# Round 1's first head: both weight groups in turn, seven products each

## The chip, the core and the metric

The kernel runs on one core of a Trainium2 chip. TensorE multiplies matrices into PSUM banks; VectorE (DVE in the profile), ScalarE (ACT) and GpSimd (POOL) work elementwise; SyncE (SP) issues the transfers between memory and the core. Each engine takes its instructions in the order in which the program lists them for it, and waits on semaphores for the others. The metric is the device time of one execution in microseconds, the median of several runs.

## The reference

A decoder layer on 2048 positions (and 16 learned meta tokens ahead of them) of width 1024. In all matters here:

```python
hn = rms_norm(h, norm_g)
proj = hn @ w_in                        # 1024 -> 8 x 512: cx, cb, cc, cg, q, k, v, rg
conv_out = short_conv_branch(cx, cb, cc, conv_w) * silu(cg)
ret = head_group_norm(retention_chunkwise(rotary(q) * d**-0.5, rotary(k), v), ret_norm_g)
mixed = concat([conv_out, ret * silu(rg)])
h = rms_norm(h + mixed @ w_out, final_g)
```

The retention has four heads of 128 and works in chunks of 128 positions; the convolution branch is worked in four groups of 128 channels.

## The kernel before

**Rounds and units.** The positions are worked in two rounds of 1024 (`r` = 0, 1). A round goes through eight units (`UNITS`): four heads (`head`) and four convolution groups (`conv_group`; the first of round 0 is `group_plain`). Each unit has two weight groups of four 128x512 blocks. For a head these are keys and values, then queries and the output gate. Round 0 ends with the convolution group 7, round 1 starts with head 0.

**Three matmuls for one.** All operands are fp32 and are split into a rounded high part and a remainder. `split` does it: ScalarE casts the high part (`wh` for a weight, `mh` for an activation), VectorE subtracts it from the source (`wl`, `ml`). Each 128x128 by 128x512 product then takes three matmuls, low by high, high by low, high by high.

**Seven products for eight.** `quad` multiplies a 2x2 block of weights by a 2x2 block of activations with seven block products instead of eight. A product is four steps along the depth of three matmuls each, 12 matmuls. It needs four activation blocks (`m[0]` to `m[6]`, one slot for each; some are inputs x, others sums T of x blocks which were worked out and stored during round 0 and are loaded again) and one weight block. Weight splits go through a ring of three buffers (`RING`), so a weight can be split only when the product three before it is done. `take` adds up the results in two PSUM banks. In round 1 the weight sums of most groups are loaded from `sums_a`, where round 0 stored them: seven blocks for a group and not four. `quad_plain` is the direct form with eight products, 96 matmuls, from four weight blocks that have a slot of their own.

**Head 0 of round 1.** The loop at the end (`else` branch, L1139 on) loads and scales all sixteen x blocks (`moving`), splits four plain weight blocks, and loads the sums of two slots. `head` works keys and values with `quad_plain`, as `first` holds something there; it then loads the sums of the other slots (`rest_of_sums`), stores the last convolution group's result (`kept`), and works queries and gate with `quad`. After a result of keys or queries is in (`take`), `rotary` turns it on VectorE in four steps, two of them on half of the partitions. Values and keys are split into 16-bit planes on ScalarE, transposed by a transfer, and joined again (`part`, `join`, `join_keys`).

**The order.** The code names the work; a scheduler places it on each engine by readiness and by the order of the code, and `tc.issue_after` keeps a piece behind a named instruction. In the texts below, K0 to K6 and Q0 to Q6 are the seven products of the key-value and the query group of this head in their new form, and L0 to L6 the products of the last weight group of round 0.

Of the kernel before, what the change touches and what calls it, by code (L numbers as in the profile page):

```python
# [8 lines left out]
F32 = mybir.dt.float32  # L9
# [6 lines left out]
P = 128  # L16
# [6 lines left out]
HB = 512  # L23
# [3 lines left out]
KH = KT // 2  # L27
# [51 lines left out]
def hybrid_trunk(ctx: ExitStack, tc: tile.TileContext, t, out: bass.AP, chunk_decay):  # L79
# [47 lines left out]
    def add(eng, out, a, b):  # L127
        eng.tensor_tensor(out=out, in0=a, in1=b, op=ALU.add)  # L128
# [53 lines left out]
    def moving(load, scale=None, after={}, behind={}):  # L182
# [11 lines left out]
                    after.get((j, k), lambda: None)()  # L194
        return m, blocks

    def block_sums(b11, b12, b22, b21, t1, t3, f, g):
# [14 lines left out]
        sub(nc.vector, t3, b22, b11)  # L212
# [10 lines left out]

    loaded = [None]

    def prepared(m, src, ns, held={}):

        for n in ns:
            for kt in range(KH):
                a = held.get((n, kt))  # L230
                if a is None:
                    a = gen("t")[:, :HB]
                    loaded[0] = nc.sync.dma_start(a, src[n, kt])
                parts(m, SUMS[n], kt, a)

    def idle():
# [4 lines left out]
    def quad(w, m, take, steps=()):  # L241


        steps = iter(steps)

        def product(i, bank, first):
            (wh, wl) = w[i]
            for kt in range(KH):
                ks = slice(kt * P, (kt + 1) * P)
                mh, ml = m[i][kt]  # L250
                for n, (a, b) in enumerate(((wl, mh), (wh, ml), (wh, mh))):
                    nc.tensor.matmul(  # L252
                        bank, a[:, ks], b, start=first and kt == 0 and n == 0, stop=kt == KH - 1 and n == 2,
                        skip_group_check=not first,
                    )
# [29 lines left out]
        take(1, 0, xb, None)  # L285

    def plain_part(n, load, slot):
        a = sb.tile([P, HB], F32, name="ra", tag="ra", bufs=RAW)
# [175 lines left out]
    def load_x(r):  # L464
        def load(k, j):
            a = gen("x")[:, :HB]
            if r == 0:
                in_line(a, t["xT"][r, j, k])
            else:
                nc.sync.dma_start(a, t["xT"][r, j, k])  # L470
            return a

        return load
# [76 lines left out]
    def w_loads(n, r=0):  # L550
# [4 lines left out]
        return [lambda a, b=b: nc.sync.dma_start(a, b) for b in blocks]  # L555

    def kept_sums(n, r):
        return sums_a[n] if r == 0 and n in KEPT else None

    mixed = [  # L560
        dram.tile([2, 2, 2, P, KH, P], F32, name=f"mixed{b}", tag=f"mixed{b}") for b in range(SEQ // HB)
# [87 lines left out]
    def conv_group(g, r, m, f, blocks, ahead, steps=(), last=False):  # L649
# [34 lines left out]
        cs = [taps(u[j], g) for j in range(2)]  # L684
        gates = []

        def gated():
            j, c = gates.pop()
            nc.scalar.activation(c, c, AF.Silu)  # L689
            mul(nc.gpsimd, cs[j], cs[j], rr[j])  # L690
            mul(nc.gpsimd, cs[j], cs[j], c)

        def take(i, j, pp, c):
            if i == 0:
                add(nc.vector, c, pp, c)
# [8 lines left out]
            taken[0] = nc.vector.tensor_tensor(out=cs[j], in0=pp, in1=cs[j], op=ALU.mult)  # L704
# [4 lines left out]
        def store():  # L709
            for j in range(2):  # L710
                store_mixed(r, j, g, cs[j])

        if last:
            kept.append(store)
        else:
            store()
        return blocks
# [23 lines left out]
    def part(a, to_cross=None):  # L741

        apart, across = gen("pl")[:, :HB], gen("tr")[:, :HB]
        nc.scalar.copy(out=planes(apart), in_=halves(a))
        if to_cross is None:
            cross(across, apart)
        else:
            to_cross.append((across, apart))
        return across

    waiting = [[], []]

    def catch_up(stage):

# [10 lines left out]
    def head(h, r, m, rot_t, f, turning, blocks, ahead, sums, first=(), between=((), idle, idle, idle)):  # L765
# [1 line left out]

        to_cross, queried = [], []  # L770
# [5 lines left out]
        def take(i, j, pp, c):  # L776
            if i == 1 and c is None:
                v[j] = part(pp, to_cross if len(first) else None)
                return
            d = gen("kv")[:, :HB]  # L780
            if c is None:
                nc.scalar.copy(out=d, in_=pp)
            else:
                add(nc.vector, d, pp, c)
            if i == 0:
                rotary(d, tables[j])
                k[j] = d
            else:
                v[j] = d
                late.append(j)  # L790

        if len(first) > 0:
            quad_plain(first[0], m, take)
        else:
            with tc.issue_after(spreading[0].ins) if r + h == 0 else nullcontext():
                w = stationary(blocks[0], nc.vector if r + h == 0 else nc.gpsimd, kept_sums(2 * h, r))
            quad(w, m, take, between[0] or (finish_late,))
            catch_up(0)
        between[1]()
        if to_cross:  # L800
            with tc.issue_after(loaded[0].ins):
                for pair in to_cross:
                    cross(*pair)
        q, sg = [None, None], [None, None]

        def take(i, j, pp, c):
            d = gen("qg")[:, :HB]
            if i == 0:
                if c is None:
                    nc.scalar.copy(out=d, in_=pp)  # L810
                else:
                    add(nc.vector, d, pp, c)
                rotary(d, tables[j])
# [11 lines left out]
        def split_keys(j):  # L825
            across_k[j] = part(k[j])
# [5 lines left out]
        def split_late():  # L832
            for j in late:
                v[j] = part(v[j])
            split_keys(0)

        def join(j):
# [15 lines left out]
            join_keys(0)  # L853
            between[3]()

        quad(stationary(load_raw(w_loads(2 * h + 1, r)), keep=kept_sums(2 * h + 1, r)), m, take, (split_late, middle, late_middle))
        with tc.issue_after(copied[0].ins):
            join(1)
            weigh(1)
            join_keys(1)  # L860
        between[2]()
        with tc.issue_after(queried[0].ins):
            next(sums, None)
# [191 lines left out]
    for r in range(NR):  # L1055
# [7 lines left out]
        if r == 0:  # L1063
# [70 lines left out]
                            parts(m, i, kt, held[kt])  # L1134

            between = (), idle, idle, idle
            later = prepare(load_x(1), sums_x, gain_of)
        else:
            m, b = moving(load_x(r), gain_of)  # L1139
            first = [plain_parts(w_loads(0))]  # L1140
            load_tables()
            prepared(m, sums_x, (1, 3))

            def rest_of_sums():
                prepared(m, sums_x, (0, 2))
                with tc.issue_after(loaded[0].ins):
                    kept.pop()()

            between = (), rest_of_sums, idle, idle
# [74 lines left out]
```

## Time and profile before

| | |
|---|---|
| median of 3 runs | 867.62 us (867.51 to 868.01) |
| profiled execution | 867.66 us, of which the span is 865.9 |
| weight loads (PEld) | 705.7 us busy |
| VectorE | 683.0 us busy |
| ScalarE | 499.0 us busy |
| GpSimd | 288.7 us busy |
| DMA | 154.43 MB, mean 178 GB/s |

The span is the time from the first to the last instruction of the profiled execution. A busy time is a sum over an engine's instructions, which overlap with those of other engines. The page also cuts the span into 40 slices of 21.6 us; the digits are tenths of a slice:

```profile
PE   8999999999999999999999999999999999999996
DVE  6798989889897977979677787976655699767663
ACT  7875648474855654948374757544433565555553
DMA  8736357566777744966365657547344584455441
```

The change touches the seventeenth to nineteenth slice, from about 345 to 410 us.

### The profile page before, as it was taken

The numbers are of one execution on the slowest core, as the hardware profiler recorded it, in microseconds if no ns is written. First come the engines' busy times: TensorE is split into PE (matmuls) and PEld (weight loads), VectorE is DVE, ScalarE is ACT, GpSimd is POOL, SyncE is SP. The second block draws the span as 40 slices with busy tenths as digits, with TensorE's granted clock in tenths as the row PEclk, the third lists the DMA queues.
The fourth block names the chain that finished last, engine by engine and source line by source line (L and its number), as shares of the span: only waits on it lengthen the run. The fifth ranks groups of instructions, "written<-read, shape, count | busy, mean of one in ns | idle before, by whom it ended". The sixth has DMA issues, their size and how long they took to land.

```text
span 865.9 us, 12846 instructions
## 1 busy us (share of the span) xinstructions
PE 854.1 (99%) x4216; PEld 705.7 (82%) x4216; DVE 683.0 (79%) x1204; ACT 499.0 (58%) x901; POOL 288.7 (33%) x226
## 2 busy tenths in 40 slices
PE   8999999999999999999999999999999999999996
PEld 6778888878887778788888888888888888888885
DVE  6798989889897977979677787976655699767663
ACT  7875648474855654948374757544433565555553
POOL 0022232422255554320000002341312154777773
PEclk9999999999999999999999999999999999999999
DMA  8736357566777744966365657547344584455441
GB/s 294 252 142 159 96 145 210 149 185 193 183 233 242 243 147 158 338 197 163 81 171 178 162 194 167 186 135 256 97 122 122 205 318 146 162 181 169 146 139 68
DMA packets 141187, 154.43 MB, mean 178 GB/s; under 512 B 59904, under 2 KB 77632, under 8 KB 141120
## 3 DMA queue, kind: packets, MB, share of 16 engines
q1 hardware_dynamic: 140544, 153.21, 57.8%
q8 instruction: 33, 0.54, 0.3%
q10 hardware_dynamic: 576, 0.40, 0.1%
q14 instruction: 34, 0.28, 0.1%
HBM read 101.14 MB, written 39.85 MB: 163 GB/s over the span
## 4 chain that ended last, share of the span: by engine, by line
PE 93%; DVE 3%; issue 1%; DMA 1%; POOL 0%; ACT 0%; POOLq 0%; SPq 0%; DVEq 0%
PE pj L252 75%; PE pj L309 5%; PE pj L333 5%; PE ms L902 2%; PE ms L891 2%; PE ms L901 2%; PE ms L878 2%; PE ms L506 1%; DVE wl L120 1%; DMA ra<-in_w_in 1%; DVE ml L123 0%; DMA gain<-in_norm_g 0%; DVE qg L931 0%; DVE x L205 0%; DVE c L581 0%
## 5 line engine op out<-in xcount | busy, mean ns | idle before, releaser
L252 PE MATMUL pj<-mh,wl 128*128 128x512 f32 x1008 | 395.7, 393 | 0.5 <-DVE wl L120 0.5
L252 PE MATMUL pj<-mh,wh 128*128 128x512 f32 x1008 | 393.2, 390 | 0.0
L252 PE MATMUL pj<-ml,wh 128*128 128x512 f32 x1008 | 392.7, 390 | 0.0
L119 ACT CAST wh<-ra 128x512 fp32r<-128x512 f32 x229 | 142.3, 621 | 250.3 <-PE pj L252 210.6
L120 DVE TENSOR_TENSOR wl<-ra,wh 128x512 fp32r<-128x512 f32 x229 | 188.3, 824 | 59.4 <-ACT wh L119 58.2
L252 PEld LDWEIGHTS pj<-mh,wl 128*128 128x128 f32 x1008 | 189.3, 188 | 41.1 <-issue 1.1
L252 PEld LDWEIGHTS pj<-mh,wh 128*128 128x128 f32 x1008 | 189.3, 188 | 39.4
L252 PEld LDWEIGHTS pj<-ml,wh 128*128 128x128 f32 x1008 | 189.4, 188 | 38.1
L131 POOL TENSOR_TENSOR ra<-ra 128x512 f32<-128x512 f32 x44 | 69.0, 1567 | 78.7 <-PE ms L506 38.3
L914 POOL TENSOR_TENSOR rp<-rs,neg_half 128x4 f32<-128x4 f32 x16 | 18.8, 1173 | 151.5 <-DVE rs L128 151.4
L259 ACT COPY tc<-pj 128x512 f32<-128x512 f32 x108 | 62.6, 580 | 0.2
L128 POOL TENSOR_TENSOR sa<-ra 128x512 f32<-128x512 f32 x22 | 33.2, 1508 | 59.2 <-DMA ra<-in_w_in 38.2
L663 POOL TENSOR_TENSOR c<-c,tc 128x512 f32<-128x512 f32 x14 | 26.1, 1862 | 47.7 <-ACT tc L689 47.7
L131 POOL TENSOR_TENSOR ra<-sa,ra 128x512 f32<-128x512 f32 x22 | 31.7, 1440 | 30.5 <-DVE wl L120 20.6
L977 DVE TENSOR_TENSOR yo<-pj,yo 128x512 f32<-128x512 f32 (+1 forms) x33 | 21.9, 671 | 17.5 <-PE pj L252 8.8
L663 POOL TENSOR_TENSOR c<-c,rr 128x512 f32<-128x512 f32 x14 | 22.3, 1592 | 36.9 <-DVE c L704 25.0
L988 POOL TENSOR_TENSOR z<-yo,final_g 128x512 f32<-128x512 f32 x16 | 27.1, 1692 | 19.4 <-DVE yo L977 19.4
L128 DVE TENSOR_TENSOR tc<-pj,tc 128x512 f32<-128x512 f32 x28 | 19.2, 684 | 14.6 <-PE pj L252 14.6
L918 DVE TENSOR_SCALAR pm<-ms,mv,rp 128x128 f32<-128x128 f32 x64 | 21.8, 404 | 10.2 <-POOL rp L914 10.2
L123 DVE SCALAR_TENSOR_TENSOR ml<-x,gain,mh 128x512 fp32r<-128x512 f32 x32 | 24.7, 809 | 5.6 <-ACT mh L122 5.4
L128 POOL TENSOR_TENSOR yo<-yo,tc 128x512 f32<-128x512 f32 x18 | 26.0, 1454 | 3.4 <-ACT tc L259 3.2
L581 DVE SCALAR_TENSOR_TENSOR c<-u,conv_w,c 128x512 f32<-128x512 f32 x32 | 25.2, 830 | 2.3 <-POOL u L572 1.2
(161 smaller groups left out, 1214.0 us busy)
## 6 DMA issues: line engine op xcount, KB each, us to landing
ra<-in_w_in SPq DMA_DIRECT2D x111, 256.0 KB, 2.9
ra<-sums_a SPq DMA_DIRECT2D x52, 256.0 KB, 2.9
x<-in_xT SPq DMA_DIRECT2D x48, 256.0 KB, 5.0
sums_a<-ra SPq DMA_DIRECT2D x42, 256.0 KB, 2.1
w<-in_w_out SPq DMA_DIRECT2D x32, 256.0 KB, 5.0
ra<-mixed SPq DMA_DIRECT2D x32, 256.0 KB, 2.8
yo<-in_x SPq DMA_DIRECT2D x32, 256.0 KB, 4.4
ra<-in_x SPq DMA_DIRECT2D x16, 256.0 KB, 3.5
```

Source lines behind the costliest of these rows:

```text
L119: nc.scalar.copy(out=hi, in_=src)
L120: lowered[0] = eng.tensor_tensor(out=lo, in0=src, in1=hi.bitcast(F32), op=ALU.subtract)
L123: nc.vector.scalar_tensor_tensor(out=lo, in0=src, scalar=scale, in1=hi.bitcast(F32), op0=ALU.mult, op1=ALU.subtract)
L128: eng.tensor_tensor(out=out, in0=a, in1=b, op=ALU.add)
L131: eng.tensor_tensor(out=out, in0=a, in1=b, op=ALU.subtract)
L252: nc.tensor.matmul(bank, a[:, ks], b, start=first and kt == 0 and n == 0, stop=kt == KH - 1 and n == 2, skip_group_check=not first,)
L259: copied[0] = nc.scalar.copy(out=c, in_=bank)
L309: nc.tensor.matmul(banks[i], a[:, ks], b, start=half + kt + n == 0, stop=half == 1 and kt == KH - 1 and n == 2,)
L333: nc.tensor.matmul(banks[n][i], a[:, ks], b, start=half + kt + s == 0, stop=half == 1 and kt == KH - 1 and s == 2,)
L581: nc.vector.scalar_tensor_tensor(out=c, in0=u[:, tap : tap + HB], scalar=conv_w[:, g, tap : tap + 1], in1=c, op0=ALU.mult, op1=ALU.add)
L663: eng.tensor_tensor(out=out, in0=a, in1=b, op=ALU.mult)
L988: nc.gpsimd.tensor_tensor(out=ys[i][j], in0=y, in1=final_g[:, j * HB : (j + 1) * HB], op=ALU.mult)
```

## The change

Keys and values of round 1's first head are worked in seven products like all the others, and in turn with the queries: K0, Q0, K1, Q1 and so on, two banks for each of the two groups. The new function `quads` does it; `weights_in_turn` loads each weight block just ahead of its split, and `moving_in_turn` loads only the twelve x blocks that seven products need. All these loads stand in one line (`in_line`), in the order of their use. The steps between the pairs of products prepare the blocks of later ones.

```diff
+    def moving_in_turn(load, scale, sums):
...
+        blocks(0, 0)
+        with tc.issue_after(copied[0].ins):
+            blocks(1, 0)
+        steps = [
+            lambda: sums(m, 1), lambda: sums(m, 0), lambda: sums(m, 2), lambda: blocks(1, 1), lambda: sums(m, 3),
+        ]
+        return m, steps
...
+    def quads(ws, m, takes, between=()):
...
+        for i in range(7):
+            for n, take in enumerate(takes):
+                if i < 2:
+                    banks[n][i] = ps_proj()
+                bank = banks[n][1 if i in (1, 3, 5) else 0]
+                product(n, i, bank, i in (0, 1, 3))
+                if i == 0:
+                    copies[n] = copy(bank)
+                elif i == 1:
+                    take(0, 0, bank, copies[n])
...
+            next(between, idle)()
...
+    def weights_in_turn(n, r):
+        for load in w_loads(n, r, in_line):
+            a = raw()
+            load(a)
+            yield weight_parts(a)
```

In `conv_group` the last group of round 0 no longer gates its result at once. `gate_late` does it, and it is called after the blocks of T2 are split, with two GpSimd products where there were four:

```diff
+        def gate_late():
+            for j, gate in enumerate(ungated):
+                mul(nc.vector, gate, gate, rr[j])
+                nc.scalar.activation(gate, gate, AF.Silu)
+                mul(nc.vector, cs[j], cs[j], rr[j])
+                mul(nc.gpsimd, cs[j], cs[j], gate)
+            return store
...
-            m, b = moving(load_x(r), gain_of)
-            first = [plain_parts(w_loads(0))]
+            m, first = moving_in_turn(load_x(r), gain_of, lambda m, n: prepared(m, sums_x, (n,), in_turn=True))
             load_tables()
-            prepared(m, sums_x, (1, 3))
-
-            def rest_of_sums():
-                prepared(m, sums_x, (0, 2))
+
+            def open_sums(t2=first[0], t1=first[1]):
+                t2()
+                with tc.issue_after(lowered[0].ins):
+                    store_kept = kept.pop()()
+                t1()
+                early.append(lowered[0])
+                return store_kept
```

`early` keeps the first rotary of keys and of queries behind the T1 blocks (`m[3]`). In `head`, the transposes of values and keys and the joins move with it, to behind the products:

```diff
+        if len(first) > 0:
+            steps = first[:3] + [lambda: (first[3](), split_keys(0)), idle, split_values, lambda: split_keys(1)]
+            quads([weights_in_turn(2 * h + n, r) for n in range(2)], m, (take_keys, take_queries), steps)
+            join_keys(0)
+            join(1)
+            weigh(1)
+            join(0)
+            weigh(0)
+            join_keys(1)
```

Where the instructions stand shows at two places. On TensorE at the seam of the rounds, where `pj_3735` is a bank of the last group and `pj_4040` one of the plain keys, the order before was:

```order
L252 MATMUL pj_3735<-ml43_747,wh_3719 128x512
L252 MATMUL pj_3735<-mh43_746,wh_3719 128x512
L309 MATMUL pj_4040<-mh00_3871,mh30_3967 128x512
L309 MATMUL pj_4040<-mh00_3871,ml30_3968 128x512
L309 MATMUL pj_4040<-ml00_3872,mh30_3967 128x512
```

The first 24 matmuls of the plain keys stood between L4 and L5. Now:

```order
L272 MATMUL pj_3735<-ml43_747,wh_3719 128x512
L272 MATMUL pj_3735<-mh43_746,wh_3719 128x512
L272 MATMUL pj_3806<-mh50_275,wl_3728 128x512
L272 MATMUL pj_3806<-ml50_276,wh_3727 128x512
L272 MATMUL pj_3806<-mh50_275,wh_3727 128x512
```

L5 follows L4 directly, and K0 comes after L6. The second place is VectorE between Q1 and K2, where `qg_4057` is the addition that reads the bank of Q1, `kv_4031` are the keys, `ml4` are blocks for K4 and Q4, and `wl_4091` is the weight of K2. The rows now:

```order
L128 TENSOR_TENSOR qg_4057<-pj_4038,tc_3954 128x512
L816 TENSOR_TENSOR kv_4031<-kv_4031,rot_4033 128x512
L813 TENSOR_TENSOR rot_4059<-qg_4057,rot_t_3862 64x512
L814 TENSOR_TENSOR rot_4059<-qg_4057,rot_t_3862 64x512
L120 TENSOR_TENSOR ml40_4067<-t_4064,mh40_4066 128x512
L815 TENSOR_TENSOR qg_4057<-qg_4057,rot_t_3862 128x512
L120 TENSOR_TENSOR ml41_4073<-t_4070,mh41_4072 128x512
L120 TENSOR_TENSOR ml42_4079<-t_4076,mh42_4078 128x512
L816 TENSOR_TENSOR qg_4057<-qg_4057,rot_4059 128x512
L120 TENSOR_TENSOR ml43_4085<-t_4082,mh43_4084 128x512
L120 TENSOR_TENSOR wl_4091<-ra_4088,wh_4090 128x512
```

Before, at the addition of the query group's product 1 (`qg_4286`), the weights of the products 2, 3 and 4 (the last is `wl_4243`) stood ahead of it:

```order
L120 TENSOR_TENSOR wl_4239<-ra_4218,wh_4238 128x512
L120 TENSOR_TENSOR ml32_4175<-t_4172,mh32_4174 128x512
L120 TENSOR_TENSOR ml33_4181<-t_4178,mh33_4180 128x512
L120 TENSOR_TENSOR ml40_4187<-t_4184,mh40_4186 128x512
L120 TENSOR_TENSOR wl_4243<-ra_4220,wh_4242 128x512
L120 TENSOR_TENSOR ml41_4193<-t_4190,mh41_4192 128x512
L128 TENSOR_TENSOR qg_4286<-pj_4273,tc_4267 128x512
```

So the weight of the next product has moved from ahead of that addition to ten rows behind it.

More of the change, by code (lines that the diff above doesn't have):

```diff
@@ L195, in moving, with blocks @@
         return m, blocks
+    def moving_in_turn(load, scale, sums):
+        m = [[] for _ in range(8)]
+        def blocks(half, j):
+            for kt in range(KH):
+                k = half * KH + kt
+                parts(m, BLOCK[half][j], kt, load(k, j), scale(k) if scale else None)
+        blocks(0, 0)
[5 more added lines that the diff above has]
+        return m, steps
     def block_sums(b11, b12, b22, b21, t1, t3, f, g):
@@ L224, in hybrid_trunk, with prepared @@
     loaded = [None]
-    def prepared(m, src, ns, held={}):
+    def prepared(m, src, ns, held={}, in_turn=False):
         for n in ns:
@@ L232, in prepared @@
                     a = gen("t")[:, :HB]
-                    loaded[0] = nc.sync.dma_start(a, src[n, kt])
+                    if in_turn:
+                        in_line(a, src[n, kt])
+                    loaded[0] = line[0] if in_turn else nc.sync.dma_start(a, src[n, kt])
                 parts(m, SUMS[n], kt, a)
@@ L285, in quad, with product, copy @@
         take(1, 0, xb, None)
+    def quads(ws, m, takes, between=()):
+        between = iter(between)
+        banks = [[None, None] for _ in ws]
+        copies = [None for _ in ws]
+        def product(n, i, bank, first):
+            wh, wl = next(ws[n])
+            for kt in range(KH):
+                ks = slice(kt * P, (kt + 1) * P)
+                mh, ml = m[i][kt]
+                for s, (a, b) in enumerate(((wl, mh), (wh, ml), (wh, mh))):
+                    nc.tensor.matmul(
+                        bank, a[:, ks], b, start=first and kt == 0 and s == 0, stop=kt == KH - 1 and s == 2,
+                        skip_group_check=not first,
+                    )
+        def copy(bank):
+            c = sb.tile([P, HB], F32, name="tc", tag="tc", bufs=COPIES)
+            copied[0] = nc.scalar.copy(out=c, in_=bank)
+            return c
+        for i in range(7):
[8 more added lines that the diff above has]
+                    take(0, 0, bank, copies[n])
+                elif i == 2:
+                    copies[n] = [copy(bank)]
+                elif i == 3:
+                    copies[n].append(copy(bank))
+                elif i == 4:
+                    take(1, 1, bank, copies[n][1])
+                elif i == 5:
+                    take(0, 1, bank, copies[n][0])
+                else:
+                    take(1, 0, bank, None)
+            next(between, idle)()
     def plain_part(n, load, slot):
@@ L462, in in_line, with load_x @@
             line[0] = nc.sync.dma_start(out, src)
-    def load_x(r):
+    def load_x(r, first=True):
         def load(k, j):
             a = gen("x")[:, :HB]
-            if r == 0:
+            if first:
                 in_line(a, t["xT"][r, j, k])
@@ L548, in hybrid_trunk, with w_loads @@
     KEPT = [n for n in range(4 * NG) if n // 2 != NG]
-    def w_loads(n, r=0):
+    def w_loads(n, r=0, load=nc.sync.dma_start):
         if r and n in KEPT:
@@ L554, in w_loads @@
             blocks = [t["w_in"][n, i] for i in range(4)]
-        return [lambda a, b=b: nc.sync.dma_start(a, b) for b in blocks]
+        return [lambda a, b=b: load(a, b) for b in blocks]
     def kept_sums(n, r):
         return sums_a[n] if r == 0 and n in KEPT else None
+    def weights_in_turn(n, r):
[3 more added lines that the diff above has]
+            yield weight_parts(a)
     mixed = [
@@ L685, in conv_group @@
         gates = []
+        ungated = []
         def gated():
+            if last:
+                return
             j, c = gates.pop()
@@ L694, in take @@
             if i == 0:
+                if last:
+                    gate = brief("cg")
+                    add(nc.vector, gate, pp, c)
+                    ungated.append(gate)
+                    return
                 add(nc.vector, c, pp, c)
@@ L711, in store @@
                 store_mixed(r, j, g, cs[j])
+        def gate_late():
[5 more added lines that the diff above has]
+            return store
         if last:
-            kept.append(store)
+            kept.append(gate_late)
         else:
@@ L739, in cross, with part @@
         )
-    def part(a, to_cross=None):
+    def part(a):
         apart, across = gen("pl")[:, :HB], gen("tr")[:, :HB]
         nc.scalar.copy(out=planes(apart), in_=halves(a))
[L745 to L748, printed above, removed]
+        cross(across, apart)
         return across
-    waiting = [[], []]
+    waiting, early = [[], []], []
     def catch_up(stage):
@@ L765, in head @@
     def head(h, r, m, rot_t, f, turning, blocks, ahead, sums, first=(), between=((), idle, idle, idle)):
-        to_cross, queried = [], []
+        queried = []
         k, v, late = [None, None], [None, None], []
@@ L774, in head, with take_keys @@
         tables = [rot_t[:, :, j * HB : (j + 1) * HB] for j in range(2)]
-        def take(i, j, pp, c):
+        def take_keys(i, j, pp, c):
             if i == 1 and c is None:
-                v[j] = part(pp, to_cross if len(first) else None)
+                v[j] = part(pp)
                 return
@@ L785, in take @@
             if i == 0:
-                rotary(d, tables[j])
+                with queued(early if j == 0 and len(first) else ()):
+                    rotary(d, tables[j])
                 k[j] = d
@@ L790, in take, with take_queries @@
                 late.append(j)
[L792 to L803, printed above, removed]
         q, sg = [None, None], [None, None]
-        def take(i, j, pp, c):
+        def take_queries(i, j, pp, c):
             d = gen("qg")[:, :HB]
@@ L812, in take @@
                     add(nc.vector, d, pp, c)
-                rotary(d, tables[j])
+                with queued(early if j == 0 and len(first) else ()):
+                    rotary(d, tables[j])
                 queried.append(turned[0])
@@ L830, in join_keys, with split_values, split_late @@
             nc.scalar.copy(out=halves(kt[j]), in_=planes(across_k[j]))
-        def split_late():
+        def split_values():
             for j in late:
                 v[j] = part(v[j])
+        def split_late():
+            split_values()
             split_keys(0)
@@ L854, in late_middle @@
             between[3]()
-        quad(stationary(load_raw(w_loads(2 * h + 1, r)), keep=kept_sums(2 * h + 1, r)), m, take, (split_late, middle, late_middle))
-        with tc.issue_after(copied[0].ins):
+        if len(first) > 0:
+            steps = first[:3] + [lambda: (first[3](), split_keys(0)), idle, split_values, lambda: split_keys(1)]
+            quads([weights_in_turn(2 * h + n, r) for n in range(2)], m, (take_keys, take_queries), steps)
+            join_keys(0)
             join(1)
             weigh(1)
+            join(0)
+            weigh(0)
             join_keys(1)
+        else:
+            with tc.issue_after(spreading[0].ins) if r + h == 0 else nullcontext():
+                w = stationary(blocks[0], nc.vector if r + h == 0 else nc.gpsimd, kept_sums(2 * h, r))
+            quad(w, m, take_keys, between[0] or (finish_late,))
+            catch_up(0)
+            between[1]()
+            w = stationary(load_raw(w_loads(2 * h + 1, r)), keep=kept_sums(2 * h + 1, r))
+            quad(w, m, take_queries, (split_late, middle, late_middle))
+            with tc.issue_after(copied[0].ins):
+                join(1)
+                weigh(1)
+                join_keys(1)
         between[2]()
@@ L1136, in hybrid_trunk, with close_sums @@
             between = (), idle, idle, idle
-            later = prepare(load_x(1), sums_x, gain_of)
+            later = prepare(load_x(1, False), sums_x, gain_of)
         else:
-            m, b = moving(load_x(r), gain_of)
-            first = [plain_parts(w_loads(0))]
+            m, first = moving_in_turn(load_x(r), gain_of, lambda m, n: prepared(m, sums_x, (n,), in_turn=True))
             load_tables()
-            prepared(m, sums_x, (1, 3))
-            def rest_of_sums():
-                prepared(m, sums_x, (0, 2))
+            def open_sums(t2=first[0], t1=first[1]):
[5 more added lines that the diff above has]
+                return store_kept
+            def close_sums(t4=first[4]):
+                t4()
                 with tc.issue_after(loaded[0].ins):
                     kept.pop()()
-            between = (), rest_of_sums, idle, idle
+            first = [lambda: kept.append(open_sums()), first[2], first[3], close_sums]
+            between = (), idle, idle, idle
             blocks = None, None
```

## The prediction

> **What bounds the kernel now.** I read the page first, then the stages, then TensorE's own waits and the chain of work that ended last around the seam between the two rounds, and there VectorE's rows one by one. K0 to K6 and Q0 to Q6 are the products of the key-value and the query group of round 1's first head, L0 to L6 those of round 0's last group.
>
> ```profile
> span 865.9 us, 12846 instructions
> PE 854.1 (99%) x4216; PEld 705.7 (82%) x4216; DVE 683.0 (79%) x1204; ACT 499.0 (58%) x901; POOL 288.7 (33%) x226
> ```
>
> TensorE is busy for 854.1 of 865.9 us. Only fewer matmuls or fewer gaps in front of them can shorten the run, and any new gap adds to it in full. The seam is the tightest place, as this stage shows (length, busy time of TensorE, weight loads, VectorE, ScalarE and GpSimd, granted clock, DMA share, GB/s):
>
> ```profile
> 350.00:361.50 11.50, 10.48 (x47) 8.34 (x46) 11.50 (x16) 11.37 (x23) 3.40 (x2) 1.00 1.02 369
> ```
>
> VectorE is busy for all 11.50 us, ScalarE for 11.37, and the DMA engines are full. TensorE lost about a microsecond here; the first two rows below are its own, the rest is the chain:
>
> ```profile
> 360.02 0.39 PE L309 MATMUL pj<-mh,mh 128*128 128x512 f32 x1
> 361.42 0.50 PE L309 MATMUL pj<-mh,ml 128*128 128x512 f32 x1 [1.02 <-DVE ml L120]
> ...
> 361.42 5.74 PE pj L309 x24
> 367.17 5.44 PE pj L252 x24
> 372.61 16.09 PE pj L309 x71
> 388.70 19.04 PE pj L252 x84
> ```
>
> The first plain matmul starts at 360.02, directly behind L4. The second should follow 0.23 later and comes at 361.42: 1.2 us lost, waiting for VectorE. Then 96 plain matmuls (L309; one record is missing), L5 and L6 (24 of L252), and the query group (84) run until 407.74 (388.70 + 19.04). The 84 take 19.04, so **one matmul costs 0.227 us**, twelve of one product 2.72.
>
> **The change, part by part.** (1) *Matmuls.* 96 plain ones become 84: 12 x 0.227 = **2.7 us less** on an engine that has no slack.
>
> (2) *The old gap.* In the new order L5 follows L4, so the plain group's wait at 361.42 goes: **1.2 us less**. L5 and L6 then run from 360.02 to 360.02 + 24 x 0.227 = 365.5. Their weights are in time: L5's was done at 360.1 even before (row 359.43 below), and less stands ahead of it now. What is late next is in (3).
>
> (3) *Weights and blocks of the first products.* VectorE's prices, from rows in which it runs without a break:
>
> ```profile
> 359.43 0.68 DVE L120 TENSOR_TENSOR wl<-ra,wh 128x512 fp32r<-128x512 f32 x1
> ...
> 375.72 2.08 DVE L123 SCALAR_TENSOR_TENSOR ml<-x,gain,mh 128x512 fp32r<-128x512 f32 x3
> 377.72 0.68 DVE L704 TENSOR_TENSOR c<-pj,c 128x512 f32<-128x512 f32 x1
> ...
> 388.73 0.69 DVE L725 TENSOR_TENSOR rot<-kv,rot_t 64x512 f32<-64x512 f32 x1 [4.91 <-ACT kv L782]
> 389.43 0.69 DVE L726 TENSOR_TENSOR rot<-kv,rot_t 64x512 f32<-64x512 f32 x1
> ...
> 391.49 1.28 DVE L120 TENSOR_TENSOR ml<-t,mh 128x512 fp32r<-128x512 f32 x2
> 392.69 0.68 DVE L120 TENSOR_TENSOR wl<-ra,wh 128x512 fp32r<-128x512 f32 x1
> ```
>
> Counted from start to start, a subtraction, addition or product costs 0.60 (two from 391.49 to 392.69), the remainder of an x block 0.67 (three from 375.72 to 377.72), each of the two half-height rotary steps 0.70. ScalarE's, read in the same way:
>
> ```profile
> 365.38 1.66 ACT L119 CAST mh<-t 128x512 fp32r<-128x512 f32 x3
> 366.93 0.63 ACT L119 CAST wh<-ra 128x512 fp32r<-128x512 f32 x1
> ...
> 369.85 1.95 ACT L122 ACTIVATE mh<-x,gain 128x512 fp32r<-128x512 f32 x3
> 371.71 0.61 ACT L119 CAST wh<-ra 128x512 fp32r<-128x512 f32 x1
> ```
>
> A cast costs 0.52, an x block 0.62. L6's weight takes a ring buffer that L3 frees at 360.02 - 2.72 = 357.3. ScalarE then makes its cast, a bank's copy and the next x block, so that VectorE meets that block at about 359.0. From there to the end of K0's weight stand four x blocks (2.7), two additions, a product and three T2 blocks (six at 0.60), and the weight (0.6): 6.9, which ends at 365.9, where TensorE is ready at 365.5. To Q0's weight there are six rows (3.6, ends at 369.5), to K1's five more (3.0, ends at 372.5); TensorE needs only 2.72 for each product. K1 so starts at 372.5 and not at 365.5 + 5.45 = 371.0: **1.5 us more**, between nothing and 2.5.
>
> (4) *The rotary steps ahead of K2's weight.* This is the large term. K1 and Q1 end at 372.5 + 5.45 = 378.0. On VectorE, an engine that takes its rows in order, the addition that reads Q1's bank (`qg_4057`) cannot start before that, and K2's weight (`wl_4091`) stands ten rows behind it, while TensorE's next matmul needs `wl_4091`. Nothing else stands on TensorE in between. The eleven rows printed above are nine of 0.60 and two of 0.70, 6.8, and the last matmul is 0.39 long where the next could start after 0.23: **a wait of 7.0 us**. K2's cast on ScalarE can start when Q0 frees its buffer (369.5 + 2.72 = 372.2); with a copy and four casts ahead of it, it is done by 375.3 and does not set the wait. GpSimd may lengthen it: the two gate products that are left now fall into VectorE's break before K1's end. A case of before:
>
> ```profile
> 351.05 1.74 POOL L663 TENSOR_TENSOR c<-c,rr 128x512 f32<-128x512 f32 x1 [1.64 <-DVE c L581]
> ...
> 351.55 1.79 DVE L120 TENSOR_TENSOR wl<-sa,wh 128x512 fp32r<-128x512 f32 x1
> 353.26 0.68 DVE L128 TENSOR_TENSOR tc<-pj,tc 128x512 f32<-128x512 f32 x1
> ```
>
> The VectorE row under a running GpSimd row takes 1.7 and not 0.6. I take half of that 1.1, so **7.5 us**, with 7.0 and 8.1 as ends. Before, the same kind of addition had three further products' weights split ahead of it, 8 us of TensorE work.
>
> (5) *The clock.* No gap so long exists inside this trace; the nearest is its end, where the chain leaves TensorE for VectorE and the granted clock (third figure from the right of the stages below it) falls:
>
> ```profile
> 857.85 0.75 DVE yo L977 x2
> ...
> 862.00:863.00 1.00, 0.00 (x0) 0.00 (x0) 0.00 (x0) 0.00 (x0) 0.00 (x0) 0.84 0.86 328
> 863.00:864.00 1.00, 0.00 (x0) 0.00 (x0) 0.00 (x0) 0.00 (x0) 0.00 (x0) 0.50 0.55 197
> ```
>
> VectorE takes TensorE's last bank at 857.85, and a mean of 0.84 from 862 to 863 with 0.50 behind it puts the fall at 862.7, 4.9 us into the idle time. How long the slow pace lasts is seen at the kernel's start:
>
> ```profile
> 0.99 4.45 PE L1040 MATMUL ms<-warm 128*128 128x512 bf16 x10 [0.99 <-DVE warm L1032]
> 5.02 1.63 PE L333 MATMUL pj<-mh,mh 128*128 128x512 f32 x4
> 6.49 0.40 PE L333 MATMUL pj<-mh,ml 128*128 128x512 f32 x1
> 6.73 0.39 PE L333 MATMUL pj<-ml,mh 128*128 128x512 f32 x1
> ...
> 10.62 0.50 PE L333 MATMUL pj<-mh,mh 128*128 128x512 f32 x1 [1.21 <-ACT mh L1085]
> ```
>
> Ten matmuls take 4.03, 0.40 each, and the pace of 0.23 is there only from 6.49 on, 5.5 us after the first. A wait of 7.5 is longer than 4.9, so I expect half clock when K2 starts: 5.5 us at 0.40 hold 14 matmuls that need 3.2 at 0.227, **2.3 us more**, between nothing and 3.
>
> [...]
>
> (6) *Transfers.* Four x blocks fewer (12 for 16), three weight blocks more (14 for 11), 16 sums as before.
>
> ```profile
> 348.15 9.14 SPq L470 DMA_DIRECT2D x<-in_xT  x16
> ```
>
> At 369 GB/s 256 KB take 0.71, so the 26 up to Q2's weight, from 348.15 on, land by about 368, and K2 is wanted at 378: nothing, unless the order of arrival is upset. The queue then waits for GpSimd's gate before it stores; K4's weight behind it has more than 10 us of cover. (7) *The later gate* has two GpSimd products fewer and its VectorE work is counted in (3) and (4). (8) *After K2*: up to Q3's weight VectorE has nine rows, 5.7 us by the prices above, for 8.2 of TensorE, and the second pair of rotaries stands behind Q6's weight. The next group's first weight comes some 3 us before it is wanted, by the same prices. Nothing, or up to 4 if they slip.
>
> **Sum**: -2.7 - 1.2 + 1.5 + 7.5 + 2.3 = +7.4. The profiled execution took 867.66, 1.8 beyond its span and level with the median of 867.62. I predict 867.66 + 7.4 = **875.0 us**, rounded down.
>
> **The rivals.** *The wait without the clock's fall*: all as above but (5). For it: the 1.2 us of idle time ahead of 10.62 did not bring the slow pace back; against it the end of the run. 867.66 - 3.9 + 1.5 + 7.5 = 872.8. *Shorter wait*: nothing in (3), 7.0 less a microsecond in (4) and no fall give 869.8. *Faster*: TensorE sheds its 3.9 us and VectorE keeps ahead, because K2's weight is split before Q1 ends. Its place is row `wl_4091`, its price -3.9, so 863.8; it decides as soon as all new waits together stay under 3.9 us, and eleven rows at 0.60 behind Q1 speak against that. *A second slip*: ScalarE's copies of transposed keys and values stand ahead of the next group's casts; if they wait for the transposes, 2 to 4 us come on top, 877 to 879. That the change does not do what it says is excluded by the order: 84 matmuls stand where 96 stood.
>
> **How the numbers follow.** Forecast 0.62, no fall of the clock 0.16, shorter wait 0.05, second slip 0.12, faster 0.05. The first two and most of the slip lie between 871.0 and 878.5, some 0.87. A measurement of this kernel tells about 0.2%, 1.7 us, from no change. Of the fast case 0.04 is faster by more and 0.01 within; of the short wait 0.02 is within; the rest, 0.93, is slower.
>
> **What would show it.** Right: the gap of 7 to 8 us in front of the matmul of K2, released by the VectorE weight; a granted clock below 1 just behind it; gaps under 1 us before K0 and Q0. Wrong: no gap there, or K2's wait ended by a DMA or by ScalarE; the clock at 1.00 throughout would take 2.3 off.

## The result and the profile after

The changed kernel took 875.81 us in the median of 4 runs (875.01 to 876.38), the kernel before 867.57 in the runs beside it. The ratio is 1.0092, with a 95% interval of 1.008 to 1.0104: **8.2 us slower**. The profiled execution took 875.69 us for a span of 873.9.

The page of the changed kernel, its first lines:

```profile
span 873.9 us, 12828 instructions
PE 855.1 (98%) x4204; PEld 704.6 (81%) x4204; DVE 680.1 (78%) x1208; ACT 499.9 (57%) x901; POOL 281.9 (32%) x224
```

Twelve matmuls fewer are there (4204 for 4216), and yet TensorE is busy for 1.0 us more: some matmuls got slower. The stage in which VectorE was busy for all 11.50 us before now reads:

```profile
350.00:361.50 11.50, 11.50 (x52) 9.52 (x51) 9.63 (x16) 10.59 (x21) 0.00 (x0) 1.00 1.05 390
```

It is TensorE that has no gap here now (10.48 before), and GpSimd does nothing in it. So the tight place of the kernel before is repaired. What came instead stands some 15 us later. All waits of TensorE between 340 and 440 us (total, times, longest):

```profile
PE pj L320 <- DVE wl L120: 8.4, 3, 7.2
PE pj L272 <- ACT tc L279: 0.5, 1, 0.5
```

and the same waits in TensorE's own rows, K0, Q0 and then K2 with its neighbours:

```profile
358.87 0.39 PE L272 MATMUL pj<-mh,wl 128*128 128x512 f32 x1
...
364.08 0.39 PE L272 MATMUL pj<-mh,wh 128*128 128x512 f32 x1
365.11 0.50 PE L320 MATMUL pj<-mh,wl 128*128 128x512 f32 x1 [0.64 <-DVE wl L120]
...
368.73 0.50 PE L320 MATMUL pj<-mh,wl 128*128 128x512 f32 x1 [0.60 <-DVE wl L120]
...
377.10 0.39 PE L320 MATMUL pj<-mh,wh 128*128 128x512 f32 x1
384.69 0.80 PE L320 MATMUL pj<-mh,wl 128*128 128x512 f32 x1 [7.21 <-DVE wl L120]
385.29 0.63 PE L320 MATMUL pj<-ml,wh 128*128 128x512 f32 x1
385.71 0.63 PE L320 MATMUL pj<-mh,wh 128*128 128x512 f32 x1
```

Q1's last matmul starts at 377.10, K2's first at 384.69. From 385.29 on one matmul follows the other after 0.43 us instead of 0.23. VectorE's rows in that time:

```profile
377.59 0.69 DVE L128 TENSOR_TENSOR qg<-pj,tc 128x512 f32<-128x512 f32 x1
378.20 0.68 DVE L816 TENSOR_TENSOR kv<-kv,rot 128x512 f32<-128x512 f32 x1
378.92 0.69 DVE L813 TENSOR_TENSOR rot<-qg,rot_t 64x512 f32<-64x512 f32 x1
379.62 0.68 DVE L814 TENSOR_TENSOR rot<-qg,rot_t 64x512 f32<-64x512 f32 x1
380.33 0.69 DVE L120 TENSOR_TENSOR ml<-t,mh 128x512 fp32r<-128x512 f32 x1
380.94 0.68 DVE L815 TENSOR_TENSOR qg<-qg,rot_t 128x512 f32<-128x512 f32 x1
381.55 1.28 DVE L120 TENSOR_TENSOR ml<-t,mh 128x512 fp32r<-128x512 f32 x2
382.75 0.68 DVE L816 TENSOR_TENSOR qg<-qg,rot 128x512 f32<-128x512 f32 x1
383.35 0.68 DVE L120 TENSOR_TENSOR ml<-t,mh 128x512 fp32r<-128x512 f32 x1
383.95 1.28 DVE L120 TENSOR_TENSOR wl<-ra,wh 128x512 fp32r<-128x512 f32 x2
```

Eleven rows without a break, from the addition that reads Q1's bank to K2's weight, the first of the two in the last line: exactly the rows that stood in the order. The granted clock over the same time (third figure from the right):

```profile
378.00:380.00 2.00, 0.00 (x0) 0.00 (x0) 1.95 (x4) 0.00 (x0) 0.00 (x0) 1.00 0.48 154
380.00:382.00 2.00, 0.00 (x0) 0.00 (x0) 1.97 (x4) 0.94 (x1) 0.00 (x0) 0.56 0.00 0
...
390.00:391.00 1.00, 1.00 (x5) 0.82 (x4) 0.00 (x0) 0.78 (x2) 0.00 (x0) 0.77 0.42 154
```

A mean of 0.56 over 380 to 382 puts the fall at 380.24, a mean of 0.77 over the microsecond from 390 the return at 390.46.

From L4's end to the next group's first matmul the profiled run of before takes 47.72 us (360.02 to 407.74), that of after 55.86 (358.87 to 414.73): 8.1 more, as much as the whole loss. The rest of the two profiled runs nearly cancels. The seam is reached 1.15 earlier in the profile of after, though TensorE's order ahead of L5 is the same; in the profiles of the kernels below that moment lies between 358.9 and 361.1, in no order that follows their edits. Behind the seam 1.0 us is lost again.

### The profile page after: what moved, and what is told of

Read it like the earlier page. It is cut to its first block, busy times and chain, and to the rows that moved or that the text cites. A ratio compares the mean times of both kernels' runs of the same rounds, so it can differ in the third digit from the quotient of the medians.

```text
span 873.9 us, 12828 instructions
## 1 busy us (share of the span) xinstructions
PE 855.1 (98%) x4204; PEld 704.6 (81%) x4204; DVE 680.1 (78%) x1208; ACT 499.9 (57%) x901; POOL 281.9 (32%) x224
## 4 chain that ended last, share of the span: by engine, by line
PE 87%; DMA 5%; DVE 4%; issue 2%; ACT 1%; POOL 0%; SPq 0%; ACTq 0%; POOLq 0%; DVEq 0%
PE pj L272 69%; PE pj L398 5%; PE pj L320 4%; PE ms L996 2%; PE ms L985 2%; PE ms L995 2%; PE ms L972 2%; PE pj L374 1%; DMA ra<-in_w_in 1%; PE ms L571 1%; DVE wl L120 1%; DMA yo<-in_x 1%; DMA t<-sums_x 1%; DMA w<-in_w_out 1%; DMA t<-sums_w 1%
## 5 line engine op out<-in xcount | busy, mean ns | idle before, releaser
L272 PE MATMUL pj<-mh,wl 128*128 128x512 f32 x980 | 385.0, 393 | 1.0 <-ACT tc L279 0.6
L272 PE MATMUL pj<-mh,wh 128*128 128x512 f32 x980 | 382.3, 390 | 0.0
L272 PE MATMUL pj<-ml,wh 128*128 128x512 f32 x980 | 381.8, 390 | 0.0
L119 ACT CAST wh<-ra 128x512 fp32r<-128x512 f32 x236 | 146.3, 621 | 255.4 <-PE pj L272 202.3
L120 DVE TENSOR_TENSOR wl<-ra,wh 128x512 fp32r<-128x512 f32 x236 | 192.7, 819 | 73.1 <-ACT wh L119 72.4
L272 PEld LDWEIGHTS pj<-mh,wl 128*128 128x128 f32 x980 | 184.0, 188 | 41.2 <-ACT tc L279 1.7
L272 PEld LDWEIGHTS pj<-mh,wh 128*128 128x128 f32 x980 | 184.0, 188 | 38.1
L272 PEld LDWEIGHTS pj<-ml,wh 128*128 128x128 f32 x980 | 184.1, 188 | 37.2
L320 PE MATMUL pj<-mh,wl 128*128 128x512 f32 x56 | 23.5, 420 | 8.4 <-DVE wl L120 8.4
L734 POOL TENSOR_TENSOR c<-c,tc 128x512 f32<-128x512 f32 x12 | 19.0, 1586 | 31.5 <-ACT tc L764 31.5
L832 ACT COPY pl<-kv 128x1024 uint16<-128x1024 uint16 x24 | 24.8, 1043 | 4.3 <-DVE ml L120 4.3
```

The lines of the kernel that those rows point to most:

```text
L119: nc.scalar.copy(out=hi, in_=src)
L120: lowered[0] = eng.tensor_tensor(out=lo, in0=src, in1=hi.bitcast(F32), op=ALU.subtract)
L272: nc.tensor.matmul(bank, a[:, ks], b, start=first and kt == 0 and n == 0, stop=kt == KH - 1 and n == 2, skip_group_check=not first,)
L320: nc.tensor.matmul(bank, a[:, ks], b, start=first and kt == 0 and s == 0, stop=kt == KH - 1 and s == 2, skip_group_check=not first,)
L734: eng.tensor_tensor(out=out, in0=a, in1=b, op=ALU.mult)
```

## The experiments

Theory: TensorE waits for the VectorE rows that stand, in order, between the addition which reads Q1's bank and K2's weight. The half clock behind that wait is a second cost of its own. Rivals: VectorE's total load, the late gate, or the transfers in one line set the loss.

**The weights split two products ahead** of their own product. K2's weight then stands ahead of Q1's addition, as before the change.

```diff
-            wh, wl = next(ws[n])
+            wh, wl = split_ahead.pop(0)
...
+        turns = iter([n for _ in range(7) for n in range(len(ws))])
+        split_ahead += [next(ws[next(turns)]) for _ in ws]
...
+                following = next(turns, None)
+                if following is not None:
+                    split_ahead.append(next(ws[following]))
```

> Only the weights are split two products ahead; the rotaries stay where they are. VectorE theory: no gap ahead of K2; twelve rows (7.4 us) now stand between the end of Q1 and K3's weight, while K2 and Q2 give 5.4 us of cover, so a gap of about 2 us ahead of K3, no fall of the clock, 867.6 us. If K2's data are late: gap and time stay at 7.2 and 875.8.

Measured: 870.29 us (10 runs), ratio 1.0026 [1.0016, 1.0035]. TensorE's waits in this kernel, K1, then K3:

```profile
371.83 0.50 PE L321 MATMUL pj<-mh,wl 128*128 128x512 f32 x1 [1.20 <-DVE wl L120]
385.81 0.60 PE L321 MATMUL pj<-mh,wl 128*128 128x512 f32 x1 [2.80 <-DVE wl L120]
```

The wait ahead of K2 is gone, and 5.5 of the 8.2 us with it. The same rotary rows now stand ahead of K3's weight and cost 2.8 there, 0.8 more than I expected. What I had not expected at all is that the clock falls on so short a gap:

```profile
386.00:387.00 1.00, 1.00 (x3) 0.76 (x3) 1.00 (x3) 1.00 (x3) 0.00 (x0) 0.53 0.00 0
...
389.00:390.00 1.00, 1.00 (x4) 0.80 (x4) 1.00 (x3) 0.62 (x2) 0.00 (x0) 0.77 0.74 193
```

Half pace from about 386.06 to 389.47: eight matmuls at 0.43 where 0.23 would do, 1.6 us. Both together are most of the miss of 2.7 us.

**The first rotary steps deferred** behind the last blocks of sums, the weights left as they were:

```diff
-                with queued(early if j == 0 and len(first) else ()):
+                if j == 0 and len(first):
+                    deferred.append(lambda: rotary(d, tables[0]))
+                else:
...
+            def turn_first():
+                first[3]()
+                with tc.issue_after(lowered[0].ins):
+                    for turning_step in deferred:
+                        turning_step()
+                queried.append(turned[0])
+                split_keys(0)
```

> Only the first rotaries move behind the last sum blocks; the weights are split as in the changed kernel. Six rows instead of eleven stand between Q1's end and K2: a gap of 3.8 us (six times 0.60 and 0.16), not 7.2. If the clock does not fall within 3.8 us: 869.6; if it falls as it did 2.8 us into the gap: 872.4. If the gap came from late data: 7.2 and 875.8 as it is.

Measured: 871.98 us (6 runs, 870.04 to 873.74), ratio 1.0047 [1.0033, 1.0061]. Its row at K2:

```profile
381.98 0.50 PE L320 MATMUL pj<-mh,wl 128*128 128x512 f32 x1 [3.86 <-DVE wl L120]
```

Fewer rows ahead of the weight, and the wait shrinks by the price of just those rows, from 7.2 to 3.9 where 3.8 was expected. The clock fell here as well, for 3.4 us from 383.1 on.

**Both together:**

> Each weight is split two products ahead of its own, and the first rotary of keys and of queries stands behind the last sum blocks. If the long gap comes from the VectorE rows between the end of Q1 and K2's weight: no gap over 1 us behind Q1, clock at 1.00 all through, 865.5 us (875.8 - 7.4 for the gap - 2.8 for the slow clock), so 2 us under the kernel before. If K2's data or casts were late: the gap stays and so does 875.8.

Measured: 865.87 us (10 runs), ratio 0.9973 [0.9964, 0.9983]: faster than the kernel before. In the profile TensorE waits around the seam for

```profile
PE pj L321 <- DVE wl L120: 1.9, 3, 1.2
```

the longest of them ahead of K1, and the granted clock is 1.00 from 340 to 440 us. The loss lay in the order of VectorE's rows. The transfers stand in one line here too, so that line does not set it. The turn of seven products need not cost time, but this run does not show that it gains any: the late gate, which is a part of this version, reaches the same time alone (below).

**The gap filled with matmuls.** 28 of the warm-up's bf16 matmuls between Q1 and K2, whose result nothing uses, keep TensorE busy in the wait:

```diff
-                    nc.tensor.matmul(
+                    multiplied[0] = nc.tensor.matmul(
...
                 elif i == 1:
+                    if n == 1:
+                        with tc.issue_after(multiplied[0].ins):
+                            warm_up(28)
                     take(0, 0, bank, copies[n])
```

> 28 matmuls on a constant, whose result nobody uses, stand on TensorE between Q1 and K2 (6.4 us); VectorE's order up to K2 is that of the changed kernel. K2 starts as late as before, but TensorE is not idle. If the slow stretch behind the gap comes from idleness: clock 1.00, 873.0 us (875.8 - 2.8). If the slow start of K2 has another cause: 875.8.

Measured: 872.77 us (4 runs), ratio 1.0054 [1.0039, 1.0069].

```profile
378.13 6.22 PE L1138 MATMUL ms<-warm 128*128 128x512 bf16 x28
385.50 0.50 PE L321 MATMUL pj<-mh,wl 128*128 128x512 f32 x1 [1.15 <-DVE wl L120]
385.84 0.40 PE L321 MATMUL pj<-ml,wh 128*128 128x512 f32 x1
386.07 0.39 PE L321 MATMUL pj<-mh,wh 128*128 128x512 f32 x1
```

K2 starts as long after Q1's last matmul as in the changed kernel, 7.6 us (377.90 to 385.50), but at the full pace of 0.23. The clock's share is 875.81 - 872.77 = **3.0 us**, by its own experiment.

**Four more VectorE rows, behind K2's weight.** They multiply the queries by a table into a tile that nothing reads.

```diff
+                    if j == 0 and len(first):
+                        spare = brief("spare")
+                        for _ in range(4):
+                            nc.vector.tensor_tensor(out=spare, in0=d, in1=tables[j][:, 0, :], op=ALU.mult)
```

> The changed kernel with four more VectorE products, computed for nothing into an unused tile: 4 x 0.60 = 2.4 us of extra work, placed behind the row of K2's weight and not ahead of it. Theory (only the rows between the addition that reads Q1's bank and K2's weight set the wait): the wait ahead of K2 stays at 7.2 us and the time at 875.8, between 875 and 877, since behind K2 VectorE has some 2.5 us of slack up to Q3's weight. Rival (VectorE's total load around the seam sets the loss): 2.4 us more, 878.2, seen as a longer wait ahead of K2 or as a new gap of 2.4 us ahead of K3.

Measured: 875.68 us (4 runs), ratio 1.0093 [1.0078, 1.0108]. VectorE's rows behind K2's weight:

```profile
384.36 0.69 DVE L120 TENSOR_TENSOR wl<-ra,wh 128x512 fp32r<-128x512 f32 x1
384.97 0.69 DVE L892 TENSOR_TENSOR spare<-qg,rot_t 128x512 f32<-128x512 f32 x1
...
391.22 0.69 DVE L892 TENSOR_TENSOR spare<-qg,rot_t 128x512 f32<-128x512 f32 x1
```

2.4 us more work on VectorE and no change in the time (875.8 to 875.7), with the wait ahead of K2 at 7.21 as before and no new wait at K3. So the load by itself is not what costs here, where VectorE has slack behind K2's weight; the place in the order is. The clock was slow for a shorter time in this profile than in that of the changed kernel, from 382.46 to 389.30, 6.8 us for 10.2:

```profile
382.00:383.00 1.00, 0.00 (x0) 0.00 (x0) 1.00 (x3) 1.00 (x2) 0.00 (x0) 0.73 0.03 8
...
389.00:390.00 1.00, 1.00 (x5) 0.79 (x5) 1.00 (x2) 0.00 (x0) 0.00 (x0) 0.85 0.48 182
```

K2 starts at 385.11 here, so 4.2 us of its work are slow and not 5.8. That is worth some 0.7 us, and the profiled seam is 0.8 shorter (55.06 for 55.86).

**The two parts of the change apart.** The turn without the late gate, by an undo of the gate's part in the changed kernel:

```diff
-            if last:
-                return
...
-                if last:
-                    gate = brief("cg")
-                    add(nc.vector, gate, pp, c)
-                    ungated.append(gate)
-                    return
...
-            kept.append(gate_late)
+            kept.append(lambda: store)
```

> The changed kernel with the gate of round 0's last group put back where it was: done at once with each bank, and only the store deferred. The turn of seven products and the loads in one line stay. Theory (the wait ahead of K2 comes from the turn alone): the wait stays at 7.2 us with K2's weight as its end, the small waits ahead of K0 and Q0 (0.6 each) change by up to 1 us in either direction since the gate's VectorE rows leave the place between K0 and Q0, and the time is 875.8, between 874.5 and 877. Rival (the late gate puts work into the break and makes part of the loss): 872 or less.

Measured: 877.13 us (4 runs, 874.95 to 878.49), ratio 1.0107 [1.0086, 1.0129]. Its two waits for weights at the seam:

```profile
367.89 0.50 PE L320 MATMUL pj<-mh,wl 128*128 128x512 f32 x1 [1.24 <-DVE wl L120]
386.27 0.80 PE L320 MATMUL pj<-mh,wl 128*128 128x512 f32 x1 [7.21 <-DVE wl L120]
```

The wait of 7.21 is there without the late gate, to the hundredth. K0 waits for longer, Q0 no more. From L5 to K2 its profiled run takes 25.2 us, that of the changed kernel 25.8. So by these two profiles the late gate costs 0.6 us up to K2 and has no part in the long wait. The median lies 0.1 above the range that was given. Whether its 1.3 us more is the gate or the spread of these four runs is left open, since the two intervals overlap.

And the late gate alone, put into the kernel before:

> The kernel before with the late gate alone: round 0's last group is gated behind T2's parts, and the first head keeps its plain and its seven-product group and its loads. Theory (the gate is worth next to nothing by itself): within 0.2% of the kernel before, 866.3 to 868.3; the gap of 1.2 us ahead of the second plain matmul may shrink, since GpSimd's products leave the place where a VectorE row took 1.7 us. Rival (the late gate itself costs several us): 870 or more, as gaps ahead of the first plain products.

Measured: 865.87 us (10 runs), ratio 0.9979 [0.997, 0.9989], 1.8 us faster than the kernel before and 0.4 below the range I had given. The second plain matmul, which waited 1.2 us before, follows its first at once (first and second plain matmul of this kernel):

```profile
359.04 0.39 PE L309 MATMUL pj<-mh,mh 128*128 128x512 f32 x1
359.26 0.39 PE L309 MATMUL pj<-mh,ml 128*128 128x512 f32 x1
```

That gap is worth 1.2 of the 1.8 us. The other 0.6 I can't place.

**The gate one step later** in the version with both edits (865.87), once behind the third blocks of sums and once ahead of them (shown is the first; in the second the two statements of `gate_then` change places):

```diff
+            def gate_then(sums=first[2]):
+                sums()
+                with tc.issue_after(lowered[0].ins):
+                    kept.append(kept.pop()())
```

> The version with weights split two products ahead and the first rotary steps deferred, and with the late gate moved one step further, behind the third blocks of sums. Three VectorE rows leave the place ahead of K1's weight. Theory (every gap left is VectorE's order of rows): the gap of 1.2 us ahead of K1 goes; K3's weight then stands some ten rows, 6.1 us, behind Q1's end, with 5.45 us of products as its cover, so a gap of about 0.7 may come there; the sum is 0.5 to 1.2 less than 865.9, that is 864.7 to 865.4, without a fall of the clock. Rival (the gap ahead of K1 is ScalarE's or a transfer's): no change, 865.9.

Measured: 870.29 us (10 runs), ratio 1.0027 [1.0017, 1.0036], a miss by 5 us. VectorE's rows there, two of the gate's four left out:

```profile
379.67 1.30 DVE L120 TENSOR_TENSOR ml<-t,mh 128x512 fp32r<-128x512 f32 x2 [1.96 <-ACT mh L119]
380.88 0.69 DVE L740 TENSOR_TENSOR cg<-cg,rr 128x512 f32<-128x512 f32 x1
...
382.69 0.69 DVE L740 TENSOR_TENSOR c<-c,rr 128x512 f32<-128x512 f32 x1
383.29 1.29 DVE L120 TENSOR_TENSOR wl<-ra,wh 128x512 fp32r<-128x512 f32 x2
```

I had counted ten rows at 0.60. But VectorE first waits 1.96 us for ScalarE's casts, and the four rows of the gate come after that break and ahead of K3's weight. TensorE waits 2.82 at K3 and the clock falls for 3.4 us. Two later waits, of 0.40 and 1.23 us, come on top. K1's gap is gone, as the theory said.

> The version with weights split two products ahead and the first rotary steps deferred, with the late gate one step later as in the run before, but ahead of the third blocks of sums and not behind them: its four VectorE rows (2.4 us) then stand ahead of the addition that reads Q1's bank, where VectorE waited 1.4 us for that bank, and no longer ahead of K3's weight. Theory (only the rows that follow the break and precede a wanted weight cost time): no gap ahead of K1, Q0 or K2; ahead of K3 0.3 us, since the casts of the third sums still end at the same time; no fall of the clock; 865.9 less the 1.9 us of its gaps, plus 0.3: 864.3, and up to 865.5 if the copies of the transposed keys slip. Rival (the rows cost the same wherever they stand around K3): a gap of 2 us or more ahead of K3, the clock falls, 869 or more.

Measured: 865.43 us (6 runs, 864.74 to 866.38), ratio 0.9969 [0.9957, 0.9981]. The same four rows ahead of the break: the only wait left at the seam is K3's, 1.48 us, and the granted clock stays at 1.00 there. That is 4.9 us less than with the rows behind the break: 1.3 at K3, 1.6 by the clock and 1.6 at the two later waits make up most of it. It missed 864.3 because K3's gap was 1.48 and not 0.3. VectorE's rows and then GpSimd's at that place:

```profile
378.18 1.79 DVE L740 TENSOR_TENSOR c<-c,rr 128x512 f32<-128x512 f32 x1
379.89 0.68 DVE L128 TENSOR_TENSOR qg<-pj,tc 128x512 f32<-128x512 f32 x1
380.50 3.56 DVE L120 TENSOR_TENSOR ml<-t,mh 128x512 fp32r<-128x512 f32 x4
```

```profile
377.81 1.61 POOL L740 TENSOR_TENSOR c<-c,cg 128x512 f32<-128x512 f32 x1 [27.41 <-ACT cg L802]
380.40 1.30 POOL L740 TENSOR_TENSOR c<-c,cg 128x512 f32<-128x512 f32 x1 [0.98 <-DVE c L740]
```

One row lasts 1.79 for 0.68, and four together 3.56 for some 2.5, each time while a GpSimd product runs: 1.1 us twice. This version (865.43), the one with both edits (865.87) and the late gate alone (865.87) are level within their spread. All three are faster than the kernel before. So the turn's twelve matmuls fewer, 2.7 us, are not seen in the time: the waits that its order still brings, 1.9 and 1.5 us, take most of them, and no run here shows a gain of the turn over the late gate alone.

## Why the prediction was right

It said 875.0 and slower; 875.81 was measured. By its steps:

(1) and (2), fewer matmuls and the old gap, -2.7 and -1.2: right. 84 matmuls stand there, and L5 to L6 run from 358.87 to 364.08 without a gap. The gap at L5 stayed away with the old gate too. In the kernel before the late gate alone would also have removed it, which I had not seen.

(3) The first weights, 1.5 predicted: 2.1 measured. K0, Q0 and K1 start 0.80, 0.76 and 0.14 late (the first is 365.11 - 364.08 - 0.23), and the first matmuls behind a wait add 0.4. VectorE is the cause that was named: their weights came each some 0.3 later than reckoned, once the earlier seam is taken off.

(4) The rows ahead of K2's weight, 7.5 predicted within 7.0 and 8.1: 7.36 measured (377.10 + 0.23 to 384.69). The rows were right, their prices nearly. The half microsecond for GpSimd was not needed: both products ran from 370.62 to 375.29, ahead of the wait. That they can cost it, 1.1 each, showed in the last experiment. Without it the sum gives 7.0, and 0.4 is missing: the eleven rows took 7.04 and not 6.8, and VectorE started on them 0.26 after TensorE could have gone on and not 0.16. So that 7.5 came this near is partly luck.

(5) The clock, 2.3 predicted: 2.8 in the trace (the 120 matmuls from 384.69 to 414.73 take 30.04 instead of 27.2), 3.0 by the filled gap. That the clock falls was right, the size was off in its parts. The fall came 2.75 us after Q1's last matmul ended (377.49) and not 4.9. The slow pace reached 5.8 us into K2, near the 5.5 that was taken, but a matmul took 0.43 there and not 0.40. The kernel's start had been misread: its matmuls follow each other after 0.43 too (1.39 to 4.80 in eight steps), and the quick pace is there from 6.02 on, hidden in the row of four, so 5.0 us after the first. The two slips cancel, as 5.0 us at 0.43 also lose 2.3. The nearness to 2.8 is luck as well: with the same gap of 7.21 the clock fell after 4.6 us and stayed low 4.2 us into K2 in the kernel with four more rows. At 0.43 for 0.227 the two stretches cost 2.7 and 2.0 us.

(6) Transfers: nothing, as said. (7) The late gate: 0.6 more up to K2 than with the old gate, by the two profiles, and open for the whole run. (8) After K2: nothing was forecast, and the next group's copy waited 0.5 for ScalarE, a loss of 0.64. ScalarE came late because it waited 0.70 for a transpose ahead of that copy. That is the second slip's mechanism in a small form.

Together: -2.7 - 1.2 + 2.1 + 7.4 + 2.8 + 0.6 is 9.0. Less 1.15 for the earlier seam and 0.3 for the slow steps behind the old gap, that gives 7.6 of the spans' 8.0. The remaining 0.4 lie outside the seam, and I can't place them. The total is nearer than its terms: the waits and the clock cost 1.6 us more than forecast, and this profile's earlier seam takes 1.15 back.

Of the rivals, *no fall of the clock* was built as the filled gap and came to 872.77, where 872.8 stood; so near it is by luck, with the terms above off by up to 0.6. *Faster* asked that K2's weight be split before Q1 ends. That alone was not enough (870.29), since the rotary rows then met K3's weight. With the rotaries deferred as well, it was, at 865.87 and not 863.8, with waits of 1.9 us left.

## What to carry to other kernels

In an in-order engine's program, list the rows between the last input that comes late and the row for which the bound engine waits; their sum was the wait here, but for some 0.2 us (a wait of 7.2 for eleven rows, of 3.9 for six), and 2.4 us more load behind the wanted row did not change it. A break of the engine itself among these rows adds to the sum, as the 1.96 us that VectorE waited for casts did. Work that nobody wants yet belongs ahead of a break in that engine and not behind it: four rows of 0.6 us moved across a break changed the time by 4.9 us, in part because the shorter gap kept the clock up. When one work order takes another's place, keep as many weights split ahead as the old one had. And measure the parts of a change alone: the late gate by itself was as fast as any version with the turn.

## What was not expected of the hardware

The clock fell on gaps of 2.80 us (the weights ahead) and 2.82 (the gate behind the third sums), and its slow stretches had three lengths: 3.4 us in these two profiles and in that with the deferred rotaries, 6.8 in the kernel with four more rows, 10.2 in the changed kernel, twice and three times as much. These last two have the same gap of 7.21. In one profile the fall came after TensorE had started again. In the kernel with the deferred rotaries K2 started at 381.98, and the clock fell at 383.1:

```profile
382.00:383.00 1.00, 1.00 (x4) 0.84 (x5) 1.00 (x2) 0.00 (x0) 0.00 (x0) 1.00 0.10 21
383.00:384.00 1.00, 1.00 (x4) 0.80 (x3) 1.00 (x3) 0.00 (x0) 0.00 (x0) 0.54 1.01 227
```

From the end of the last matmul to the fall passed 2.75 us in the changed kernel, 4.6 with four more rows and 5.0 here (378.12 to 383.08). Reckon back 3.41 us from each fall, the length of the slow stretch with the weights ahead (386.06 to 389.47): TensorE was busy there for 0.7 us in the changed kernel, for 0.6 with the weights ahead, for 1.1 here and not at all with four more rows. Gaps of 1.20 (K1 with the weights ahead), 1.20 (K1 with both edits) and 1.48 us (K3 in the last version) brought no fall.

When the clock came back, TensorE had worked without a break for 5.8 us in the changed kernel (384.69 to 390.46), for 4.2 with four more rows (385.11 to 389.30) and for 3.7 with the weights ahead (385.81 to 389.47). So the same gap of 7.21 us cost 2.7 us by the clock in one profile and 2.0 in another. No run here moved a gap on purpose, and what sets the fall and the way back was not shown.
